# The first stretch of a two-block transformer kernel: gain row between the warming matmuls, x's second tile later in the queue, two casts on GpSimd, steps in the order of k-tile pairs

## The chip, the cores and the metric

The kernel runs on one core of a Trainium2 chip. The core has five engines with queues of their own: TensorE (PE in the profile, its weight loads PEld), VectorE (DVE), ScalarE (ACT), GpSimd (POOL) and SyncE (SP, which here only starts transfers). Sixteen DMA engines move data between HBM and the on-chip memory SBUF; matmul results go to PSUM. The metric is the device time of one execution in microseconds (us), lower is better.

## The reference

Two layers of one transformer block and one layer of another run over 256 tokens of width 1024, in float32. What the change touches is the very beginning, the norm of layer 0 and the first columns of its input product:

```
def rms_norm(x, g):
    xf = x.astype(jnp.float32)
    y = xf * lax.rsqrt(jnp.mean(xf * xf, axis=-1, keepdims=True) + RMS_EPS)
    return (y * g.astype(jnp.float32)).astype(x.dtype)
...
    for l in range(DEPTH):
        h = rms_norm(x, g_pre_mix[l])
        z = h @ w_in[l]
        q, k, v, cb, cc, cx, ga, gb = jnp.split(z, splits, axis=-1)
...
        mod = jax.nn.silu(c) @ w_cond[l] + b_cond[l]
```

After that come attention, a short convolution, gates, an output product and a feed-forward part per layer, then the second block, whose modulation `mod` is computed from `c` by DVE in gaps of the first block. None of that work is changed.

## The kernel before

**Numbers as two parts.** TensorE multiplies in the type float32r. To keep float32's accuracy, each operand is split into a rounded part H and a residue L = value - H. ACT makes H (a cast), DVE makes L (a subtraction). A product is H x H, H x L and L x H. So a weight of 128x1024 (a "raw" half, 512 KB) costs one transfer by SP, one cast on ACT, one subtraction on DVE, and on PE, per tile of 128 tokens, four matmuls for its H (against both parts of x) and two for its L.

**The weight stream.** All weights lie in one packed array in the order of use. `emit_raw` issues the next raw half; there are NRAW = 7 raw buffers, so that a transfer waits until the L of the half seven before has been computed. NSPLIT = 12 pairs of H and L are held.

**Order.** A scheduler (the Tile layer) puts each engine's instructions in a fixed order when the kernel is built, about in the order of the source, and adds the waits. Each engine then runs its queue in that order; what waits holds up everything behind it. `tc.issue_after(i)` puts an instruction behind another one in that order. In the first stretch, `q_first`, the helpers `A` and `V` chain all of ACT's and DVE's work in the order in which the source calls them.

**The first stretch.** It makes q of layer 0, 1024 columns in two halves c = 0 and 1, for the token tiles t = 0 and 1:

- PE starts with WARM = 13 matmuls on a tile of ones (`warm`), which compute nothing that is used. Then the gain row `g0` (one row of 1024) is spread over all partitions by a matmul with a column of ones (`gp`, in the trace g0p), then WARM2 = 4 more warming matmuls.
- `square` sums x squared, one half of the columns on ACT (c = 0), one on DVE (c = 1); `root` adds the two and takes the power -0.5 on POOL (rs_x); `scaled` multiplies x by it and by the gain row, in pieces (xg); `turned` transposes two k-tiles of 128 columns at a time on PE (pt), a pair; `putH` and `putL` make the pair's two parts (ACT, DVE).
- `halfH` and `halfL` make H and L of a raw half of the weights (Hq, Lq). For c = 0 there are four halves, Hq0 to Hq3, numbered (h, hf); the half (h, hf) goes with pair 2h + hf of x.
- `run(t, c, h, hf, j)` is a step of PE: j = 0 with the half's H (four matmuls of 512 columns), j = 1 with its L (two).

The second raw half is held back until x's first tile has landed: a copy of one column from x into its buffer (`state["gate"]`, on DVE) must come first. x's second tile is issued before it. The table `bcol` of the second block is fetched by ACT's queue; because of where `state["dma"]` stands its issue goes to the head of that queue.

Of the kernel before, what the change touches and what calls it, by code (L numbers as in the profile page):

```python
# [12 lines left out]
AF = mybir.ActivationFunctionType  # L13
ALU = mybir.AluOpType
# [20 lines left out]
WARM = 13  # L35
WARM2 = 4
# [126 lines left out]
def tile_model(ctx: ExitStack, tc: tile.TileContext, x_in, wpack, sink, convw, gains, c_in,  # L163
# [89 lines left out]
    def emit_raw():  # L253
        i, hf = divmod(state["raw"], 2)
        t = wp.tile([P, CH // 2], F32, tag="raw", name=f"raw{i}_{hf}", bufs=NRAW)
        if state["raw"] == 1:
            state["gate"] = nc.vector.tensor_copy(t[:, 0:1], xt[0][:, 512:513])
        state["dma"] = nc.sync.dma_start(t, wpack[i][:, hf * (CH // 2):(hf + 1) * (CH // 2)])
        raws[2 * i + hf] = t
        state["raw"] += 1  # L260
# [47 lines left out]
    warm = s2("warm", (P, 512), mybir.dt.bfloat16)  # L308
# [9 lines left out]
    pw = ps1("warm_ps")  # L318
    for i in range(WARM):
        mm(pw, warm[:, 0:P], warm, i == 0, i == WARM - 1)  # L320
# [3 lines left out]
    for i in range(WARM2):  # L324
        mm(pw, warm[:, 0:P], warm, i == 0, i == WARM2 - 1)
    for i in range(3):
        emit_raw()
    nc.sync.dma_start(xt[1], x_in[P:2 * P, :])
# [5 lines left out]
    with tc.issue_after(state["gate"].ins):  # L334
        state["v"] = nc.vector.tensor_copy(ident_r, ident)
# [32 lines left out]
    def rstd(ssq, name):  # L368
        rs = small("rs_" + name, 1)
        nc.gpsimd.tensor_tensor(rs, ssq[:, 1:2], nhalf, ALU.pow)  # L370
        return rs
# [331 lines left out]
    def q_first(q, xp):  # L703
# [51 lines left out]
        def halfH():  # L755
            n = state["spl"]
            while state["raw"] <= n:
                emit_raw()
            H = wp.tile([P, CH // 2], F32R, tag="H", name=f"Hq{n}", bufs=NSPLIT)
            L = wp.tile([P, CH // 2], F32R, tag="L", name=f"Lq{n}", bufs=NSPLIT)  # L760
            A(nc.scalar.copy, H, raws[n])
            HL.setdefault(n // 2, []).append((H, L))
            hl.append((H, L))
            state["spl"] += 1
# [7 lines left out]
        def run(t, c, h, hf, j):  # L772
# [5 lines left out]
            v = w[c, h][hf][j].rearrange("p (k c) -> p k c", k=2)  # L778
# [16 lines left out]
        scaled(0, root(0), (0, 256, 512, 1024))  # L795
        halfH()
        pt = [turned(0, i) for i in range(4)]
        for i in range(2):
            putH(0, i, pt[i])
            putL(0, i, pt[i])  # L800
        halfH()
        halfL(0)
        for i in range(2, 4):
            putH(0, i, pt[i])
            putL(0, i, pt[i])
        halfL(1)
        halfH()
        square(1, 0, False)
        square(1, 1, True)
        halfL(2)  # L810
        scaled(1, root(1), (0, 256, 512, 1024))
        halfH()
        w[0, 0] = get(("q", 0, 0, 0), 4)
        w[0, 1] = get(("q", 0, 0, 1), 4)
        run(0, 0, 0, 0, 0)
        run(0, 0, 0, 1, 0)
        run(0, 0, 0, 0, 1)
        run(0, 0, 1, 0, 0)
        run(0, 0, 0, 1, 1)
        run(0, 0, 1, 0, 1)  # L820
        run(0, 0, 1, 1, 0)
        pt = [turned(1, i) for i in range(4)]
        for i in range(4):
            putH(1, i, pt[i])
            putL(1, i, pt[i])
        halfL(3)
        state["behind"] = (state["a"], state["v"])
        for h in range(2):
            for hf in range(2):
                run(1, 0, h, hf, 0)  # L830
                if h == 0:
                    run(1, 0, h, hf, 1)
        run(0, 0, 1, 1, 1)
# [9 lines left out]
    def mixer1(l, xp, norms):  # L843
# [65 lines left out]
        for c in range(2):  # L909
            nc.scalar.activation(gt["ga"][c], gt["ga"][c], AF.Sigmoid)  # L910
            nc.scalar.activation(gt["gb"][c], gt["gb"][c], AF.Sigmoid)
            nc.vector.tensor_mul(yc[c], yc[c], gt["gb"][c])
            if l == 0 and c == 0:
                csb = s4("csb")
                nc.scalar.dma_start(csb, c_in[0].partition_broadcast(P))
                with tc.issue_after(state["dma"].ins):
                    nc.scalar.dma_start(bcol, b_cond)
# [298 lines left out]
```

## Time and profile before

| what | value |
|---|---|
| median of three runs | 1149.91 us (1148.66 to 1150.13) |
| the profiled execution's time | 1148.9 us |
| its span in the trace | 1146.9 us |
| granted clock of TensorE | 0.999 |
| PE busy | 1135.7 us |
| first matmul of the second half of q | 24.04 us from the span's start |

The span runs from the first to the last recorded instruction, so the execution's own time is 2.0 us longer. A row of the time line gives start and length in us, the engine, the line of the kernel, the operation, the tiles written <- read, partitions x elements and type, a count where equal rows are merged, and in brackets how long the engine stood idle before it and what ended that. "SPq" and "ACTq" are transfers being issued by those queues; the time from issue to landing is listed apart, by tensor.

### The profile page before, as it was taken

What the parts mean: (1) busy time and instruction counts of PE and PEld (TensorE: products, weight loads), DVE (VectorE), ACT (ScalarE), POOL (GpSimd) and SP (SyncE); (2) the same over time, 40 slices, a digit from 0 to 9 for tenths busy, and PEclk for the clock granted to TensorE, in tenths of its full rate; (3) what the DMA queues carried; (4) which work ended last, traced back from release to release, by engine and by line L of the source; (5) the groups of instructions that cost most, each with busy time, mean ns of one, the idle gap of its engine ahead of it and who ended that gap; (6) DMA issues with size and microseconds to landing.
All of it is one profiled execution on the core that took longest, in us unless ns stands there. A gap on an engine that the chain in (4) does not pass through costs nothing. (4 is left out here: it accounts for less than half of the span.)

```text
span 1146.9 us, 15965 instructions
## 1 busy us (share of the span) xinstructions
PE 1135.7 (99%) x5901; PEld 951.2 (83%) x5901; DVE 799.9 (70%) x1190; ACT 686.9 (60%) x1211; POOL 13.4 (1%) x28
## 2 busy tenths in 40 slices
PE   9999999999999999999999999999999999999997
PEld 5888888888888888888888888888888777888886
DVE  7888845858977647798864758867656747865652
ACT  6777866547654446688856557545455847645441
POOL 0000000000000000000000000000000000000000
PEclk9999999999999999999999999999999999999999
DMA  8934346737987752844565538987773653855610
GB/s 299 354 129 149 127 148 203 262 140 250 355 280 238 252 203 91 295 132 153 191 220 204 184 110 287 353 260 242 256 261 108 222 166 103 307 192 183 200 62 37
DMA packets 67039, 235.39 MB, mean 205 GB/s; under 512 B 8849, under 2 KB 9361, under 8 KB 66962
## 3 DMA queue, kind: packets, MB, share of 16 engines
q1 hardware_dynamic: 63216, 224.83, 57.4%
q10 hardware_dynamic: 3746, 9.56, 2.5%
q8 instruction: 46, 0.75, 0.3%
q14 instruction: 31, 0.25, 0.1%
HBM read 233.28 MB, written 1.07 MB: 204 GB/s over the span
## 5 line engine op out<-in xcount | busy, mean ns | idle before, releaser
L280 DVE TENSOR_TENSOR L<-raw,H 128x1024 fp32r<-128x1024 f32 x370 | 444.5, 1220 | 146.8 <-ACT H L278 139.4
L278 ACT CAST H<-raw 128x1024 fp32r<-128x1024 f32 x370 | 382.9, 1052 | 140.7 <-issue 39.1
L247 PE MATMUL dn<-H,fHL 128*128 128x512 f32 x432 | 116.1, 390 | 0.0
L247 PE MATMUL pu<-xf,H 128*128 128x512 f32 x432 | 108.2, 392 | 0.0
L247 PE MATMUL pg<-xf,H 128*128 128x512 f32 x432 | 107.8, 391 | 0.0
L247 PEld LDWEIGHTS dn<-H,fHL 128*128 128x128 f32 x432 | 79.8, 188 | 15.6
L247 PEld LDWEIGHTS pg<-xf,H 128*128 128x128 f32 x432 | 79.2, 188 | 15.2
L247 PEld LDWEIGHTS pu<-xf,H 128*128 128x128 f32 x432 | 77.7, 189 | 13.9
L524 DVE SCALAR_TENSOR_TENSOR raw<-raw,silu_c 128x1024 f32<-128x1024 f32 x48 | 58.2, 1218 | 29.3 <-DMA raw<-in_wpack_dram 29.3
L247 PE MATMUL dn<-L,fHL 128*128 128x512 f32 x216 | 66.6, 389 | 0.0
L247 PEld LDWEIGHTS pg<-xf,L 128*128 128x128 f32 x432 | 58.9, 190 | 4.2
L247 PEld LDWEIGHTS pu<-xf,L 128*128 128x128 f32 x432 | 58.9, 190 | 4.2
L247 PE MATMUL pu<-xf,L 128*128 128x256 f32 x432 | 60.2, 282 | 0.0
L247 PE MATMUL pg<-xf,L 128*128 128x256 f32 x432 | 60.2, 282 | 0.0
L247 PE MATMUL wo<-H,m 128*128 128x512 f32 x192 | 52.5, 395 | 0.0
L571 ACT CAST fHL<-f 128x512 fp32r<-128x512 f32 x27 | 16.8, 621 | 57.4 <-DVE f L569 57.4
L247 PEld LDWEIGHTS dn<-L,fHL 128*128 128x128 f32 x216 | 40.5, 188 | 8.6
L565 ACT ACTIVATE s<-s 128x512 f32<-128x512 f32 x27 | 17.1, 632 | 46.6 <-DVE s L458 46.5
L247 PEld LDWEIGHTS wo<-H,m 128*128 128x128 f32 x192 | 35.4, 188 | 7.6 <-issue 0.6
L247 PE MATMUL pcp<-H,y 128*128 128x512 f32 x128 | 35.2, 395 | 0.0
L247 PE MATMUL pap<-H,o 128*128 128x512 f32 x128 | 35.1, 394 | 0.0
L666 ACT ACTIVATE P<-S,nm 128x256 f32<-128x256 f32 x64 | 29.6, 480 | 8.9 <-DVE nm L660 6.4
(290 smaller groups left out, 1934.5 us busy)
## 6 DMA issues: line engine op xcount, KB each, us to landing
raw<-in_wpack_dram SPq DMA_DIRECT2D x422, 512.0 KB, 5.2
gpm<-in_gains_dram ACTq DMA_DIRECT2D x3, 512.0 KB, 6.8
gpf<-in_gains_dram ACTq DMA_DIRECT2D x3, 512.0 KB, 8.7
gqf<-in_gains_dram ACTq DMA_DIRECT2D x2, 512.0 KB, 6.6
out_dram<-x SPq DMA_DIRECT2D x4, 256.0 KB, 2.0
pmat<-in_pmat_dram SPq DMA_DIRECT2D x2, 384.0 KB, 6.9
x<-in_x_dram SPq DMA_DIRECT2D x2, 256.0 KB, 3.1
x<-in_x_dram SPq DMA_DIRECT2D x1, 512.0 KB, 6.8
```

Source lines behind the costliest of these rows:

```text
L247: nc.tensor.matmul(o, a, b, start=start, stop=stop, **kw)
L278: nc.scalar.copy(H, r)
L280: nc.vector.tensor_sub(L, r, H.bitcast(F32))
L524: nc.vector.scalar_tensor_tensor(w[u], w[u], 1.0, silu_c, ALU.mult, ALU.mult, accum_out=mcol[:, r, 2 * j + u:2 * j + u + 1])
L565: last = nc.scalar.activation(s, s, AF.Silu)
L571: nc.scalar.copy(fHL[:, 0], fv)
L666: nc.scalar.activation(Pt[:, hh, :], S[hh // 2][:, hh % 2, :], AF.Exp, bias=nm[:, hh:hh + 1], accum_out=den[:, hh:hh + 1])
```

## The change

- Ten and two warming matmuls instead of 13 and four, so that the gain row's matmuls come after the tenth. The tile of ones is 128 wide and is read four times instead of being 512 wide.
- The copy that holds back the second raw half goes from DVE to POOL. x's second tile is issued behind the second raw half instead of before it.
- `bcol` is fetched behind the last gate's sigmoid in layer 0 instead of at the start; the identity's cast to float32r comes at the end of the stretch.
- Hq1 and Hq3 are cast by POOL instead of ACT, Hq3 behind the second tile's power.
- The steps are written by pairs: the first H step stands between the transposes of pairs 1 and 2, all H steps of tile 0 and two of its L steps come before the second tile's transposes, the other two L steps after them. On ACT the square of the second tile goes ahead of pairs 2 and 3.

```diff
@@ -32,8 +32,8 @@
 NEG = -1e30
 CH = 2048
 
-WARM = 13
-WARM2 = 4
+WARM = 10
+WARM2 = 2
 NRAW = 7
 NSPLIT = 12
 LOOK = 3
@@ -254,7 +254,7 @@
         i, hf = divmod(state["raw"], 2)
         t = wp.tile([P, CH // 2], F32, tag="raw", name=f"raw{i}_{hf}", bufs=NRAW)
         if state["raw"] == 1:
-            state["gate"] = nc.vector.tensor_copy(t[:, 0:1], xt[0][:, 512:513])
+            nc.gpsimd.tensor_copy(t[:, 0:1], xt[0][:, 512:513])
         state["dma"] = nc.sync.dma_start(t, wpack[i][:, hf * (CH // 2):(hf + 1) * (CH // 2)])
         raws[2 * i + hf] = t
         state["raw"] += 1
@@ -305,7 +305,7 @@
         q.dma_start(g, gains[i].partition_broadcast(P))
         return g
 
-    warm = s2("warm", (P, 512), mybir.dt.bfloat16)
+    warm = s2("warm", (P, P), mybir.dt.bfloat16)
     nc.vector.memset(warm, 1.0)
     for c in range(2):
         nc.sync.dma_start(xt[0][:, c * 512:(c + 1) * 512], x_in[0:P, c * 512:(c + 1) * 512])
@@ -316,23 +316,25 @@
     ones = s2("ones")
     nc.vector.memset(ones[0:1, 0:P], 1.0)
     pw = ps1("warm_ps")
+    warm4 = warm.unsqueeze(1).to_broadcast([P, 4, P])
     for i in range(WARM):
-        mm(pw, warm[:, 0:P], warm, i == 0, i == WARM - 1)
+        mm(pw.rearrange("p (a c) -> p a c", a=4), warm, warm4, i == 0, i == WARM - 1)
     gp = [ps1(f"g0p{c}") for c in range(2)]
     for c in range(2):
         mm(gp[c], ones[0:1, 0:P], g0[0:1, HC[c]], True, True)
     for i in range(WARM2):
-        mm(pw, warm[:, 0:P], warm, i == 0, i == WARM2 - 1)
-    for i in range(3):
+        mm(pw.rearrange("p (a c) -> p a c", a=4), warm, warm4, i == 0, i == WARM2 - 1)
+    for i in range(2):
         emit_raw()
-    nc.sync.dma_start(xt[1], x_in[P:2 * P, :])
+    with tc.issue_after(state["dma"].ins):
+        state["dma"] = nc.sync.dma_start(xt[1], x_in[P:2 * P, :])
+    with tc.issue_after(state["dma"].ins):
+        emit_raw()
     nhalf = cst.tile([P, 1], F32, tag="nhalf", name="nhalf")
     nc.vector.memset(nhalf, -0.5)
     eps = cst.tile([P, 1], F32, tag="eps", name="eps")
     nc.vector.memset(eps, EPS)
     ident_r = cst.tile([P, P], F32R, tag="identr", name="ident_r")
-    with tc.issue_after(state["gate"].ins):
-        state["v"] = nc.vector.tensor_copy(ident_r, ident)
     modd = dr.tile([6, D], F32, tag="modd", name="modd")
     mcol = cst.tile([P, 6, KT], F32, tag="mcol", name="mcol")
     bcol = cst.tile([P, 6, KT], F32, tag="bcol", name="bcol")
@@ -367,7 +369,7 @@
 
     def rstd(ssq, name):
         rs = small("rs_" + name, 1)
-        nc.gpsimd.tensor_tensor(rs, ssq[:, 1:2], nhalf, ALU.pow)
+        state["pow"] = nc.gpsimd.tensor_tensor(rs, ssq[:, 1:2], nhalf, ALU.pow)
         return rs
 
     class Norm:
@@ -752,13 +754,16 @@
 
         hl = []
 
-        def halfH():
+        def halfH(pool=False):
             n = state["spl"]
             while state["raw"] <= n:
                 emit_raw()
             H = wp.tile([P, CH // 2], F32R, tag="H", name=f"Hq{n}", bufs=NSPLIT)
             L = wp.tile([P, CH // 2], F32R, tag="L", name=f"Lq{n}", bufs=NSPLIT)
-            A(nc.scalar.copy, H, raws[n])
+            if pool:
+                nc.gpsimd.tensor_copy(H, raws[n])
+            else:
+                A(nc.scalar.copy, H, raws[n])
             HL.setdefault(n // 2, []).append((H, L))
             hl.append((H, L))
             state["spl"] += 1
@@ -775,7 +780,7 @@
                 ps[t, c] = ps1(f"pq_0{c}{t}")
                 ps[t, c, "n"] = 0
             ts_ = slice(t * P, (t + 1) * P)
-            v = w[c, h][hf][j].rearrange("p (k c) -> p k c", k=2)
+            v = (w[c, h] if c else hl[2 * h:])[hf][j].rearrange("p (k c) -> p k c", k=2)
             first = ps[t, c, "n"] == 0
             ps[t, c, "n"] += 1
             for k in range(2):
@@ -792,44 +797,51 @@
         w = {}
         square(0, 0, False)
         square(0, 1, True)
-        scaled(0, root(0), (0, 256, 512, 1024))
+        rs = root(0)
+        scaled(0, rs, (0, 256, 512))
         halfH()
-        pt = [turned(0, i) for i in range(4)]
         for i in range(2):
-            putH(0, i, pt[i])
-            putL(0, i, pt[i])
-        halfH()
+            pt = turned(0, i)
+            putH(0, i, pt)
+            putL(0, i, pt)
+        run(0, 0, 0, 0, 0)
+        scaled(0, rs, (512, 1024))
+        halfH(True)
         halfL(0)
+        square(1, 0, False)
         for i in range(2, 4):
-            putH(0, i, pt[i])
-            putL(0, i, pt[i])
-        halfL(1)
-        halfH()
-        square(1, 0, False)
-        square(1, 1, True)
-        halfL(2)
-        scaled(1, root(1), (0, 256, 512, 1024))
-        halfH()
-        w[0, 0] = get(("q", 0, 0, 0), 4)
-        w[0, 1] = get(("q", 0, 0, 1), 4)
-        run(0, 0, 0, 0, 0)
+            pt = turned(0, i)
+            putH(0, i, pt)
+            putL(0, i, pt)
         run(0, 0, 0, 1, 0)
         run(0, 0, 0, 0, 1)
+        square(1, 1, True)
+        rs = root(1)
+        halfH()
+        halfL(1)
+        with tc.issue_after(state["pow"].ins):
+            halfH(True)
         run(0, 0, 1, 0, 0)
+        run(0, 0, 1, 1, 0)
         run(0, 0, 0, 1, 1)
-        run(0, 0, 1, 0, 1)
-        run(0, 0, 1, 1, 0)
+        scaled(1, rs, (0, 256, 512, 1024))
         pt = [turned(1, i) for i in range(4)]
         for i in range(4):
             putH(1, i, pt[i])
             putL(1, i, pt[i])
+            if i == 1:
+                halfL(2)
         halfL(3)
+        V(nc.vector.tensor_copy, ident_r, ident)
         state["behind"] = (state["a"], state["v"])
         for h in range(2):
             for hf in range(2):
                 run(1, 0, h, hf, 0)
                 if h == 0:
                     run(1, 0, h, hf, 1)
+        for h in range(2):
+            get(("q", 0, 0, h), 4)
+        run(0, 0, 1, 0, 1)
         run(0, 0, 1, 1, 1)
         run(1, 0, 1, 0, 1)
         run(1, 0, 1, 1, 1)
@@ -908,12 +920,12 @@
         drain()
         for c in range(2):
             nc.scalar.activation(gt["ga"][c], gt["ga"][c], AF.Sigmoid)
-            nc.scalar.activation(gt["gb"][c], gt["gb"][c], AF.Sigmoid)
+            sig = nc.scalar.activation(gt["gb"][c], gt["gb"][c], AF.Sigmoid)
             nc.vector.tensor_mul(yc[c], yc[c], gt["gb"][c])
             if l == 0 and c == 0:
                 csb = s4("csb")
                 nc.scalar.dma_start(csb, c_in[0].partition_broadcast(P))
-                with tc.issue_after(state["dma"].ins):
+                with tc.issue_after(sig.ins):
                     nc.scalar.dma_start(bcol, b_cond)
                 nc.scalar.activation(silu_c, csb, AF.Sigmoid)
                 nc.vector.tensor_mul(silu_c, silu_c, csb)
```

On SP the issues stand as follows before (from the second on; raw_0 and raw_1 are the two halves of a weight chunk, x_73 is its second tile):

```order
L258 DMA raw_0_106<-in_wpack_dram 128x1024
L328 DMA x_73<-in_x_dram 128x1024
L258 DMA raw_1_108<-in_wpack_dram 128x1024
L258 DMA raw_0_111<-in_wpack_dram 128x1024
L258 DMA raw_1_197<-in_wpack_dram 128x1024
```

and now:

```order
L258 DMA raw_0_101<-in_wpack_dram 128x1024
L258 DMA raw_1_103<-in_wpack_dram 128x1024
L330 DMA x_73<-in_x_dram 128x1024
L258 DMA raw_0_107<-in_wpack_dram 128x1024
L258 DMA raw_1_198<-in_wpack_dram 128x1024
```

x's tile moved behind the second raw half, the one that waits for the copy from x's first tile.

On ACT, from the first square on, before (with the tiles' numbers: jk and sx belong to the squares, Hq are weights, the x are the pairs of both tiles):

```order
L708 ACTIVATE jk_139,sx_135<-x_72 128x512
L708 ACTIVATE sx_135<-sx_135,eps 128x1
L708 CAST Hq_150<-raw_0_106 128x1024
L708 CAST x_165<-pt_153 128x2x128
L708 CAST x_168<-pt_156 128x2x128
L708 CAST Hq_171<-raw_1_108 128x1024
L708 CAST x_175<-pt_159 128x2x128
L708 CAST x_178<-pt_162 128x2x128
L708 CAST Hq_182<-raw_0_111 128x1024
L708 ACTIVATE jk_185,sx_136<-x_73 128x512
```

and now:

```order
L710 ACTIVATE jk_133,sx_129<-x_72 128x512
L710 ACTIVATE sx_129<-sx_129,eps 128x1
L710 CAST Hq_143<-raw_0_101 128x1024
L710 CAST x_149<-pt_146 128x2x128
L710 CAST x_155<-pt_152 128x2x128
L710 ACTIVATE jk_168,sx_130<-x_73 128x512
L710 ACTIVATE sx_130<-sx_130,eps 128x1
L710 CAST x_174<-pt_171 128x2x128
L710 CAST x_180<-pt_177 128x2x128
L710 CAST Hq_194<-raw_0_107 128x1024
```

The second tile's square (reading x_73) moved ahead of the casts of pairs 2 and 3, and Hq1 left the queue.

On POOL, after the fills at the start, before (rs_x are the two tiles' powers; ISA is an instruction that the scheduling layer inserts ahead of the first power):

```order
L1212 UNCONDITIONAL_BRANCH
L370 ISA
L370 TENSOR_TENSOR rs_x_145<-sx_135,nhalf 128x1
L370 TENSOR_TENSOR rs_x_192<-sx_136,nhalf 128x1
L370 TENSOR_TENSOR rs_apm_2504<-sa_pm_2476,nhalf 128x1
```

and now:

```order
L1224 UNCONDITIONAL_BRANCH
L257 COPY raw_1_103<-x_72 128x1
L372 ISA
L372 TENSOR_TENSOR rs_x_139<-sx_129,nhalf 128x1
L764 CAST Hq_164<-raw_1_103 128x1024
L372 TENSOR_TENSOR rs_x_192<-sx_130,nhalf 128x1
L764 CAST Hq_200<-raw_1_198 128x1024
L372 TENSOR_TENSOR rs_apm_2499<-sa_pm_2471,nhalf 128x1
```

The copy from x's first tile now stands ahead of the ISA instruction and the powers, and the two casts stand behind one power each.

## The prediction

> **What bounds the kernel now.** I read the page first, then the waits of TensorE (PE), then stretches of the first 60 us, then the first 25 us instruction by instruction. The page's first line, then four stretches (from:to, length, busy time with count of PE, PEld, DVE, ACT and POOL, granted clock, DMA share, GB/s):
>
> ```profile
> PE 1135.7 (99%) x5901; PEld 951.2 (83%) x5901; DVE 799.9 (70%) x1190; ACT 686.9 (60%) x1211; POOL 13.4 (1%) x28
> ...
> 0.00:8.99 8.99, 7.54 (x21) 2.74 (x22) 3.34 (x14) 3.35 (x5) 0.76 (x5) 1.00 0.77 259
> 8.99:16.80 7.81, 6.93 (x31) 4.76 (x30) 6.32 (x13) 5.04 (x10) 0.55 (x1) 1.00 1.00 385
> 16.80:24.04 7.24, 6.99 (x35) 5.72 (x34) 7.00 (x11) 6.58 (x11) 0.00 (x0) 1.00 0.69 238
> 24.04:60.00 35.96, 35.96 (x187) 30.50 (x186) 30.03 (x46) 27.26 (x40) 0.00 (x0) 1.00 0.92 338
> ```
>
> PE is busy 99% of the span, and from 24.04 us on without a break. So the change, which acts before that point, is worth exactly what it moves the start of the second column half of q (24.04 us), as long as weights, casts and residues stay ahead behind it. Before 24.04 PE is not full. Its rows (start, length, operation):
>
> ```profile
> 6.21 1.98 PE L247 MATMUL g0p<-g,ones 1*128 1x512 f32 x4
> 8.12 1.04 PE L247 MATMUL warm_ps<-warm 128*128 128x512 bf16 x4
> 8.99 1.04 PE L742 MATMUL pt<-ident,xg 128*128 128x128 f32 x8
> 15.30 0.74 PE L247 MATMUL pq<-Lq,x 128*128 128x512 f32 x2 [0.79 <-DVE Lq L713]
> 16.80 0.61 PE L742 MATMUL pt<-ident,xg 128*128 128x128 f32 x4
> 17.66 0.63 PE L742 MATMUL pt<-ident,xg 128*128 128x128 f32 x4 [0.25 <-DVE xg L713]
> 18.04 1.17 PE L247 MATMUL pq<-Hq,x 128*128 128x512 f32 x4
> 20.87 1.98 PE L247 MATMUL pq<-Hq,x 128*128 128x512 f32 x8
> 22.68 1.52 PE L247 MATMUL pq<-Lq,x 128*128 128x512 f32 x6
> 24.04 1.07 PE L247 MATMUL pq<-H,x 128*128 128x512 f32 x4
> ```
>
> From starts: eight H matmuls 20.87 to 22.68, so an H step (four) is 0.905; six L matmuls 22.68 to 24.04, so an L step (two) is 0.453. A group of eight transposes is 0.85 (8.99 to 9.84 by starts; 1.24 at 16.80, of which 0.25 waits); I take 1.0. The first half of q holds 8 H steps, 8 L steps and 16 transposes: 7.24 + 3.62 + 2.0 = 12.9 us. From 8.99 to 24.04 are 15.05, so about 2.2 us are idle or slow. That is all there is to fill behind the first transpose; ahead of it the whole start can move too.
>
> What feeds PE there: the transfers, and ACT, DVE and POOL.
>
> ```profile
> 1.65 0.43 SPq L258 DMA_DIRECT2D raw<-in_wpack_dram  x1
> 1.69 0.44 ACTq L917 DMA_DIRECT2D bcol<-in_b_cond_dram  x1
> 2.12 0.43 SPq L328 DMA_DIRECT2D x<-in_x_dram  x1
> 4.81 21.62 SPq L258 DMA_DIRECT2D raw<-in_wpack_dram  x15
> ```
>
> Median us from issue to landing for single issues: the first raw (at 1.65), x's tile two (at 2.12), the second raw (at 4.81); then the smallest, median and largest of the raws of the first 40 us.
>
> ```profile
> raw<-in_wpack_dram SPq DMA_DIRECT2D x1, 512.0 KB, 6.0
> x<-in_x_dram SPq DMA_DIRECT2D x1, 512.0 KB, 6.8
> raw<-in_wpack_dram SPq DMA_DIRECT2D x1, 512.0 KB, 5.4
> DMA to landing us min/median/max: 4.4/6.6/9.5
> ```
>
> So raw 0 lands at 7.65, x's tile two at 8.9, raw 1 at 10.2.
>
> ```profile
> 0.34 0.10 POOL L1205 MEMSET const-uint8-127<- 128x1 uint8 x1
> 0.91 0.48 DVE L309 MEMSET warm<- 128x512 bf16 x1 [0.91 <-PEq L1205]
> 4.62 0.15 DVE L257 COPY raw<-x 128x1 f32<-128x1 f32 x1 [3.06 <-DMA x<-in_x_dram]
> 4.83 0.23 DVE L335 CAST ident_r<-ident 128x128 fp32r<-128x128 f32 x1
> 4.97 0.68 DVE L713 SCALAR_TENSOR_TENSOR jk<-x 128x512 f32<-128x512 f32 x1
> 5.77 0.16 DVE L713 TENSOR_TENSOR sx<-sx 128x1 f32<-128x1 f32 x1
> 6.01 0.55 POOL L370 TENSOR_TENSOR rs_x<-sx,nhalf 128x1 f32<-128x1 f32 x1 [5.57 <-DVE sx L713]
> 7.43 1.54 DVE L713 SCALAR_TENSOR_TENSOR xg<-x,rs_x,g0p 128x256 f32<-128x256 f32 x3 [1.50 <-PE g0p L247]
> 7.67 1.05 ACT L708 CAST Hq<-raw 128x1024 fp32r<-128x1024 f32 x1 [3.11 <-DMA raw<-in_wpack_dram]
> 9.41 0.65 ACT L708 CAST x<-pt 128x256 fp32r<-128x256 f32 x2 [0.69 <-PE pt L742]
> 9.81 0.76 DVE L713 TENSOR_TENSOR x<-pt,x 128x256 fp32r<-128x256 f32 x2 [0.84 <-ACT x L708]
> 10.49 1.21 DVE L713 TENSOR_TENSOR Lq<-raw,Hq 128x1024 fp32r<-128x1024 f32 x1
> 12.69 0.64 ACT L708 ACTIVATE jk<-x 128x512 f32<-128x512 f32 x1
> 13.65 1.03 ACT L708 CAST Hq<-raw 128x1024 fp32r<-128x1024 f32 x1
> ```
>
> The first xg waits for the gain row's matmul (1.50), not for rs (ready at 6.56). The square of x's tile two starts at 12.69 without a wait: its data had been there since 8.9.
>
> **The change part by part.**
>
> *Warm-ups.* Three of 13 fall before the gain row, at 0.22 each by the second group (8.12 to 8.99, four): g0p starts at 5.55 instead of 6.21. The smaller memset brings PE's start 0 to 0.42 forward (0.48 down to no less than a 128x1 fill's 0.10, rounded); I take nothing. Then xg can start at 5.55 + 1.22 = 6.77 (7.43 less 6.21), the two later warm-ups end at 5.55 + 1.91 + 0.44 = 7.9, and the first transposes start there, 1.1 earlier than 8.99. rs must be ready at 6.7: without gate copy and identity cast in DVE's way the sum of squares starts at 4.62, 0.35 earlier, so rs comes at about 6.2.
>
> *What the early start reaches.* DVE's new order puts the second half of xg behind two residues: casts of pairs 0 and 1 at 7.9 + 0.42 = 8.3, residues at 8.7 to 9.5, the last xg piece to 10.2 (0.75), its transposes, and the cast of pair 2 at 10.65 at the earliest.
>
> *x's tile two, fourth.* Now it stands behind raw 1, which waits for a copy on POOL. That copy starts at 4.62 as DVE's did; between POOL's 128x1 rows (0.10 and 0.55) against DVE's 0.15, raw 1 is issued at 4.8 to 5.2, nearest 4.85. x follows 0.43 later, at 5.28. With the 5.4 of the raw issued at 4.81 it lands at 10.7; with 4.4 and 6.8 as ends, 9.65 to 12.45. Call it X. ACT now squares x ahead of the casts of pairs 2 and 3, so ACT stands still from about 8.9 to X, and with it everything behind in its queue: the sum of squares' second part, both casts, the third H.
>
> *The chain from X.* 0.96 on ACT (12.69 to 13.65), cast of pair 2 at X+1.0, residues 0.40 later and 0.76 long: X+2.15. DVE's square and sum 0.80 (4.97 to 5.77): X+2.95. POOL's power after 0.24, 0.55 long: X+3.75. Then the fourth H, cast by POOL: no row shows a 128x1024 cast there. Ends: 0.55 (POOL's 128x1 power) and 2.4 (twice DVE's two-operand 1.21); nearest in kind is ACT's same cast, 1.05, so I take 1.2. X+5.0. PE's H step on it, the L step of raw 1, the transposes of tile two: 0.905 + 0.453 + 1.0, X+7.4. Behind them stand 4 H and 6 L steps (before: 4 and 5), 3.62 + 2.72: the second half of q starts at X+13.75. xg of tile two is ready at about X+5.8 (behind L of raw 1, X+4.3) and does not add.
>
> X = 10.7 gives 24.45 against 24.04: **0.4 us later**. The other chain (cast of pair 2 at 10.65, so X replaced by 9.65) gives 23.4, so 0.65 earlier is the best this order allows with these durations.
>
> *At nothing:* bcol's issue (0.44 at 1.69) leaves an ACT that waits for x until 4.6 at worst anyway, and lies later beside a 60% busy ACT; ident_r's cast (0.23) moves behind the last L, before its first use by the key transposes; two casts fewer on ACT (2 x 1.05) free an engine that waits for X. Raw buffers come free later by 1 to 2 us; the second half needs one raw per 2.7 us of PE, and DMA then moves 338 GB/s, 1.6 us a raw. If that cover were gone, PE would wait in the stretch from 24.04, which has no wait now.
>
> [...] The power of tile two now starts 0.2 us after L of raw 1, a DVE operation with two SBUF inputs. In the one overlap here POOL was not held up, but there one input was in PSUM:
>
> ```profile
> 254.26 0.55 POOL L370 TENSOR_TENSOR rs_apm<-sa_pm,nhalf 128x1 f32<-128x1 f32 x1 [4.92 <-ACT sa_pm L365]
> 254.31 0.41 DVE L212 TENSOR_TENSOR xf<-pt_nf,xf 128x256 fp32r<-128x256 f32 x1
> ```
>
> The sum above goes by this row. [...]
>
> The profiled execution took 1148.9 (span 1146.9), 1.0 under the median of 1149.91. With 0.4 on top: 1149.3, or 1150.3 against the median. 0.2% (2.3 us) is about what a measurement of this kernel can tell from no change.
>
> **The rivals.**
>
> 1. *PE is filled.* If x lands about when it did (8.9) and POOL's casts take half of ACT's, PE could run from 7.9 nearly without a gap: 7.9 + 12.9 = 20.8, 3.2 earlier: **1146.7**. For it: all the earlier pieces are ready sooner. Against: the order on DVE and ACT alone holds the point to 23.4. It needs those chains to be shorter than their rows.
>
> 2. *POOL is held by DVE.* Power waits until L of raw 1 ends, X+4.3 instead of X+3.2, and the fourth H follows: 1.05 more, 25.5: **1151.4**.
>
> 3. *x lands early, the order decides:* 23.4, **1149.3**.
>
> 4. *Slower: what POOL does unseen.* Ahead of the first power POOL's queue holds an instruction (named ISA in the order) that the trace does not show. Before, it lies in POOL's 5.57 us of idle time, and the power starts 0.08 after the sum's end at 5.93. So it takes anything from 0 to 5.3. Now the gate copy stands ahead of it, and it cannot start before 4.85. Up to 1.3 it costs nothing, up to about 2.4 X hides it; beyond that each microsecond counts. At 5.3 rs is ready at 10.7 instead of 6.2, xg starts 3.95 later than 6.77, and the best chain goes from 23.4 to 27.4: 3.35 over 24.04, **1153.3**. For it: the instruction is there and moved behind a wait. Against: the power was not even 0.1 late at 6.01, which asks for a coincidence if it is long. [...]
>
> **How the numbers follow.** The forecast, X between its ends without hold: 0.42, **1150.3**, its own range 1149.3 to 1152.1. Held POOL 0.20, early x 0.12, filled PE 0.14, the unseen instruction 0.12. Faster by over 0.2% is the filled PE and a little of the early x: 0.16. Slower is the unseen instruction (long enough) and the top of the held one: 0.15. The rest is the same, 0.69. The range reaches halfway into the filled PE and to the unseen instruction's price: 1147.0 to 1153.2.
>
> **What would show it.** In the changed kernel's trace: g0p near 5.6 and the first transposes near 7.9; ACT idle before its second square, ended by DMA x, until about 10.7; POOL's two casts near 1.2; the second half of q near 24.5. Power of tile two starting only when L ends would show the second rival; the first power later than 7, the fourth. A square of tile two that does not wait, with PE dense from 8, makes me wrong on the fast side. Behind that point PE should stay without a wait to 60 us.

## The result and the profile after

In 20 runs of each, the kernel before took 1149.34 us (median; 1147.93 to 1152.12) and the changed one 1152.02 us (1149.39 to 1153.36): ratio 1.0020, 95% interval 1.0013 to 1.0027. The change makes the kernel slower, by 2.7 us between the medians and by 2.3 us (1.5 to 3.1) by the ratio, which is not the quotient of the medians here or below. The forecast was +0.4, and the time lies inside the range given. The profiled execution of the changed kernel took 1151.74 us and has a span of 1149.5 us (before 1146.9), with a mean granted clock of 0.996 (before 0.999).

First the page's line of busy times and the waits of PE over 0.7 us (us in total, times, longest), both of the changed kernel:

```profile
PE 1137.6 (99%) x5896; PEld 952.6 (83%) x5896; DVE 801.5 (70%) x1189; ACT 685.9 (60%) x1209; POOL 17.1 (1%) x31
```

```profile
PE pq L247 <- ACT Hq L710: 1.6, 1, 1.6
PE warm_ps L247 <- DVE warm L309: 1.1, 1, 1.1
PE pq L642 <- DVE qs L637: 0.8, 1, 0.8
PE pq L247 <- POOL Hq L764: 0.7, 1, 0.7
```

The first and the fourth are new, and both lie in the first half of q. Stretches of the first 60 us, cut where the working of the prediction cut them, the third at the start of the second half of q:

```profile
0.00:8.99 8.99, 7.69 (x23) 3.21 (x24) 3.10 (x14) 4.00 (x7) 1.46 (x6) 1.00 0.67 215
8.99:16.80 7.81, 5.36 (x18) 2.91 (x17) 6.38 (x11) 2.59 (x6) 3.50 (x3) 0.84 1.01 373
16.80:27.06 10.26, 10.26 (x41) 8.46 (x40) 7.42 (x11) 7.67 (x11) 0.00 (x0) 0.79 0.60 201
27.06:60.00 32.94, 32.94 (x167) 27.70 (x166) 27.75 (x43) 24.58 (x37) 0.00 (x0) 1.00 0.95 346
```

The second half of q starts at 27.06 instead of 24.04, 3.0 later, and PE is full behind it, as before. The spans differ by 2.6: nothing is added later, and some 0.4 is made up. Two things are new in these rows. From 8.99 to 16.80 PE works 5.36 us instead of 6.93. And the third number from the end, the granted clock, is 0.84 and 0.79, where before it was 1.00 everywhere. The rows of the time line in that stretch:

```profile
4.47 0.71 POOL L257 COPY raw<-x 128x1 f32<-128x1 f32 x1 [4.03 <-DMA x<-in_x_dram]
4.78 1.98 PE L247 MATMUL g0p<-g,ones 1*128 1x512 f32 x4
5.49 0.55 POOL L372 TENSOR_TENSOR rs_x<-sx,nhalf 128x1 f32<-128x1 f32 x1 [0.31 <-DVE sx L715]
5.58 0.43 SPq L330 DMA_DIRECT2D x<-in_x_dram  x1
7.13 0.60 PE L744 MATMUL pt<-ident,xg 128*128 128x128 f32 x4
9.05 1.04 POOL L764 CAST Hq<-raw 128x1024 fp32r<-128x1024 f32 x1 [3.01 <-DMA raw<-in_wpack_dram]
9.28 1.89 DVE L715 TENSOR_TENSOR Lq<-raw,Hq 128x1024 fp32r<-128x1024 f32 x1
10.34 0.63 ACT L710 ACTIVATE jk<-x 128x512 f32<-128x512 f32 x1 [2.14 <-DMA x<-in_x_dram]
12.36 0.68 DVE L715 SCALAR_TENSOR_TENSOR jk<-x 128x512 f32<-128x512 f32 x1
13.08 0.16 DVE L715 TENSOR_TENSOR sx<-sx 128x1 f32<-128x1 f32 x1
13.16 1.23 DVE L715 TENSOR_TENSOR Lq<-raw,Hq 128x1024 fp32r<-128x1024 f32 x1
13.32 1.48 POOL L372 TENSOR_TENSOR rs_x<-sx,nhalf 128x1 f32<-128x1 f32 x1 [3.23 <-DVE sx L715]
14.76 1.03 POOL L764 CAST Hq<-raw 128x1024 fp32r<-128x1024 f32 x1
15.84 2.07 PE L247 MATMUL pq<-Hq,x 128*128 128x512 f32 x4 [0.73 <-POOL Hq L764]
18.57 1.91 PE L744 MATMUL pt<-ident,xg 128*128 128x128 f32 x8
```

Read from the bottom. PE waits at 15.84 for the fourth H, which POOL casts from 14.76, because its power of 128 numbers took 1.48 us instead of 0.55 (the row at 5.49). In that time DVE computed L of raw 1 (13.16 to 14.39), which has two inputs in SBUF: the power ends 0.41 behind it. The same happens the other way round at 9.05: POOL casts until 10.09, and DVE's L, begun at 9.28, ends 1.08 later, after 1.89 instead of the 1.21 to 1.23 it takes alone. Then the last two rows: four H matmuls of 2.07 and eight transposes of 1.91, where at full clock they are 1.20 (e2 below, from 16.13) and 1.04 (before, from 8.99). The granted clock around them (again the third number from the end):

```profile
14.00:15.00 1.00, 1.00 (x4) 0.33 (x2) 0.56 (x2) 0.00 (x0) 1.00 (x2) 0.64 0.95 377
15.00:16.00 1.00, 0.27 (x2) 0.16 (x1) 1.00 (x3) 0.00 (x0) 0.79 (x1) 0.50 1.11 397
16.00:18.00 2.00, 2.00 (x5) 1.61 (x6) 0.36 (x1) 0.00 (x0) 0.00 (x0) 0.50 0.99 379
18.00:20.00 2.00, 2.00 (x9) 1.70 (x9) 0.36 (x1) 0.71 (x2) 0.00 (x0) 0.50 0.59 240
21.00:22.00 1.00, 1.00 (x5) 0.77 (x5) 1.00 (x3) 1.00 (x2) 0.00 (x0) 0.94 0.00 0
```

Taken as 1.00 up to the fall and 0.50 behind it, 0.64 is full clock for 0.28 of that microsecond, so it fell to half at 14.28; in the same way it rose at 21.12. From 15.84 the work left to the second half of q is 0.905 + 0.453 + 1.0 + 6.34 = 8.70 by the rows of before, and it took 11.22, 2.5 more. Not all of that is the clock's: in two runs below (e2 and e5) the same steps in the same order took 9.05 at full clock (16.13 to 25.18 and 16.05 to 25.10). So 2.2 us are the clock's in this execution, and without them the point would have been about 24.9, 0.85 over before.

So two theories stood: the **clock** (fewer warming matmuls and the new waits let the clock fall, and that is most of the loss), and the **chain** (x's landing, then ACT, DVE and a held POOL, set the end, whatever the clock does). Twelve further kernels were to tell them apart; they do so in part.

### The profile page after: what moved, and what is told of

The parts are those of the page before. It is cut to its first block, busy times and chain, and to the rows that moved or that the text cites. A ratio compares the mean times of both kernels' runs of the same rounds, so it can differ in the third digit from the quotient of the medians.

```text
span 1149.5 us, 15953 instructions
## 1 busy us (share of the span) xinstructions
PE 1137.6 (99%) x5896; PEld 952.6 (83%) x5896; DVE 801.5 (70%) x1189; ACT 685.9 (60%) x1209; POOL 17.1 (1%) x31
```

## The experiments

Each of the twelve was timed in 11 runs. "Over before" is the difference of the medians to the kernel before on the same chip in the same session (1149.34 to 1149.64 there). X is where the square of x's tile two starts. The last four columns are of the one profiled execution, whose own time stands first: it need not be near the median (in e4 it is 1.2 below it, in e6 and e12 1.5 and 1.7 above).

| kernel | median | over before | ratio, 95% interval | profiled execution | X | second half of q | recorded clock at 0.50 |
|---|---|---|---|---|---|---|---|
| changed | 1152.02 | +2.68 | 1.0020, 1.0013 to 1.0027 | 1151.74 | 10.34 | 27.06 | 14.3 to 21.1 |
| e1_fill | 1151.56 | +2.05 | 1.0021, 1.0012 to 1.0030 | 1151.18 | 11.29 | 25.82 | 8.0 to 11.5 |
| e2_x_early | 1151.73 | +2.22 | 1.0024, 1.0015 to 1.0033 | 1151.10 | 8.96 | 25.18 | 9.3 to 12.7 |
| e3_act_casts | 1150.25 | +0.74 | 1.0007, 0.9998 to 1.0016 | 1150.25 | 12.33 | 25.50 | 9.4 to 16.2 |
| e4_l_behind | 1150.07 | +0.56 | 1.0003, 0.9994 to 1.0012 | 1148.92 | 10.64 | 23.73 | 8.9 to 12.3 |
| e5_warm_back | 1151.56 | +1.92 | 1.0019, 1.0010 to 1.0027 | 1151.55 | 10.55 | 25.10 | none |
| e6_warm_alone | 1149.67 | +0.03 | 1.0002, 0.9993 to 1.0010 | 1151.20 | 13.75 | 25.36 | see below |
| e7_l_warm | 1149.11 | -0.53 | 1.0000, 0.9991 to 1.0009 | 1149.19 | 10.43 | 24.09 | none |
| e8_l_x_warm | 1149.19 | -0.45 | 0.9997, 0.9988 to 1.0006 | 1149.19 | 10.45 | 24.57 | none |
| e9_l_k128 | 1149.65 | +0.30 | 1.0001, 0.9992 to 1.0009 | 1148.76 | 10.67 | 23.78 | none |
| e10_l_x_k128 | 1148.81 | -0.54 | 1.0001, 0.9991 to 1.0010 | 1148.46 | 8.97 | 23.42 | none |
| e11_l_x_k128_w6 | 1149.31 | -0.04 | 1.0001, 0.9992 to 1.0010 | 1149.31 | 9.80 | 24.71 | none |
| e12_fill_warm | 1151.00 | +1.56 | 1.0014, 1.0005 to 1.0023 | 1152.68 | 12.59 | 27.18 | none |

**e1: fill PE's two waits.** Seven and five warming matmuls in the places where PE waits at 12 and 15:

```
+        fill(7)
         run(0, 0, 1, 0, 0)
+        fill(5)
         run(0, 0, 1, 1, 0)
```

> The changed kernel with 7 warming matmuls between the first L step of tile 0 and the H step on the third weight half, and 5 more ahead of the H step on the fourth; nothing else moves. Clock theory: PE's two gaps (1.64 and 0.73 us by its waits) let the granted clock fall to 0.50 from 15 to 21 us, and that costs 2.5 us. Then no stretch of the first 27 us is below clock 1.00, the second half of q starts at 15.84 + 0.905 + 0.453 + 1.0 + 6.34 = 24.5 instead of 27.06, and the time is 0.3 to 0.6 us above the kernel before, 2 to 2.5 below the changed one. Chain theory: the late x tile and the chain behind it cost the 2.7 us by themselves; then filling the gaps changes nothing, or costs a little more.

No fall of the clock behind 12 us any more, and yet only 0.6 less than the changed kernel's +2.68, with overlapping intervals. In the profile x landed 0.95 later, and the clock was at half before the filled places, from 8 us. So this run does not bear out the clock theory as stated: the waits between 12 and 16 are not the only place at which the clock falls. It does not refute it either, since the clock did fall, elsewhere.

**e2: x's tile two ahead of raw 1 again**, as in the kernel before:

```
-    for i in range(2):
-        emit_raw()
-    with tc.issue_after(state["dma"].ins):
-        state["dma"] = nc.sync.dma_start(xt[1], x_in[P:2 * P, :])
-    with tc.issue_after(state["dma"].ins):
+    for i in range(3):
         emit_raw()
+    nc.sync.dma_start(xt[1], x_in[P:2 * P, :])
```

> The changed kernel with x's second tile issued where it was, ahead of the second weight half; all else as changed. If the place of x's tile is the root: it lands at 8.9 instead of 10.3, ACT's second square does not hold up the casts of pairs 2 and 3, the third H is cast by 12.6 instead of 13.6, PE's gaps stay under 1.5 us, the clock stays at 1.00 and the second half of q starts at 22.6 to 23.4: 0.6 to 1.4 us faster than before. If the clock theory holds but the first gap (PE now waits longer for the second H, whose weights land at 10.2) is enough to drop it: slower than before by 1 to 2 us. If the place of the casts is the root: as the changed kernel, +2.7.

x no longer has to be waited for (its square starts at 8.96 without a wait), and nothing is won beyond the noise. The chain shifts to raw 1, which now lands later: POOL's cast of it holds DVE's L of raw 0 until 12.06, and DVE's queue goes on from there to the held power. (Part of the delay is the clock's, at half from 9.3 to 12.7.)

```profile
8.96 0.64 ACT L707 ACTIVATE jk<-x 128x512 f32<-128x512 f32 x1
9.95 1.04 POOL L761 CAST Hq<-raw 128x1024 fp32r<-128x1024 f32 x1 [3.62 <-DMA raw<-in_wpack_dram]
10.15 1.91 DVE L712 TENSOR_TENSOR Lq<-raw,Hq 128x1024 fp32r<-128x1024 f32 x1
13.45 1.22 DVE L712 TENSOR_TENSOR Lq<-raw,Hq 128x1024 fp32r<-128x1024 f32 x1
13.61 1.48 POOL L369 TENSOR_TENSOR rs_x<-sx,nhalf 128x1 f32<-128x1 f32 x1 [2.62 <-DVE sx L712]
16.13 1.20 PE L247 MATMUL pq<-Hq,x 128*128 128x512 f32 x4 [1.55 <-POOL Hq L761]
```

The fourth H step comes at 16.13, no earlier than in the changed kernel (15.84) although x landed at 8.6 instead of 10.3. x's place by itself is not the cause.

**e3: both casts on ACT again.** `halfH(True)` becomes `halfH()` at both places.

> The changed kernel with Hq1 and Hq3 cast by ACT again, at their places in the order. Port theory (POOL and a DVE operation with two SBUF inputs hold each other up): the first L takes 1.2 instead of 1.89, the second power 0.55 instead of 1.48, and the fourth H comes at about 14.6 instead of 15.8. With the clock theory the second gap of PE nearly closes; if the first gap (1.6) alone does not drop the clock, the second half of q starts at 23.5 to 24.0 and the time equals that of before within 0.5 us; if it does, the time is 1 to 2 us above. If the casts' place does not matter: +2.7 as the changed kernel.

The port theory, here and in e4, is the author's name for the hold in the changed kernel's rows at 9.28 and 13.32 (L 1.89 instead of 1.23, the power 1.48 instead of 0.55); that a port is behind it no run shows.

```profile
10.20 1.22 DVE L715 TENSOR_TENSOR Lq<-raw,Hq 128x1024 fp32r<-128x1024 f32 x1
15.31 1.47 POOL L372 TENSOR_TENSOR rs_x<-sx,nhalf 128x1 f32<-128x1 f32 x1 [9.22 <-DVE sx L715]
```

1.9 less than the changed kernel, with intervals that still overlap; as the clock fell, 1 to 2 over before was expected, and it is 0.74. L of raw 0 is back at 1.22, since no cast runs on POOL beside it. The expectation missed in one more point: the power still took 1.47, because L of raw 1 still stands ahead of it on DVE; but no cast queues behind the power on POOL any more. The clock was at half for longer than in any other run but the changed one (9.4 to 16.2), with x late at 12.33, and the time is still near before's. That speaks for the chain.

**e4: L of raw 1 behind xg of tile two on DVE.** One line moves (and the PE step that uses it):

```
         halfH()
-        halfL(1)
         with tc.issue_after(state["pow"].ins):
             halfH(True)
         run(0, 0, 1, 0, 0)
         run(0, 0, 1, 1, 0)
-        run(0, 0, 0, 1, 1)
         scaled(1, rs, (0, 256, 512, 1024))
+        halfL(1)
+        run(0, 0, 0, 1, 1)
```

> The changed kernel with the second L behind the second tile's xg on DVE, so that no operation with two SBUF inputs runs beside the second power (PE's order then has tile two's first transposes ahead of the fourth H step). Port theory: the second power takes 0.55 instead of 1.48, the fourth H is ready about 1 us earlier (14.8), and PE has transposes to do in the second gap. With the clock theory, if this keeps the clock up: second half of q at 23.5 to 24, equal to before within 0.6 us; if the first gap alone drops it, 1 to 2 us above before. If POOL was not held by DVE, the power takes 1.48 again and the time stays 2.7 above.

```profile
13.62 0.55 POOL L372 TENSOR_TENSOR rs_x<-sx,nhalf 128x1 f32<-128x1 f32 x1 [3.35 <-DVE sx L715]
14.13 1.04 POOL L764 CAST Hq<-raw 128x1024 fp32r<-128x1024 f32 x1
14.21 1.53 DVE L715 SCALAR_TENSOR_TENSOR xg<-x,rs_x,g0p 128x256 f32<-128x256 f32 x3 [0.67 <-POOL rs_x L372]
15.66 1.22 DVE L715 TENSOR_TENSOR Lq<-raw,Hq 128x1024 fp32r<-128x1024 f32 x1
23.73 1.07 PE L247 MATMUL pq<-H,x 128*128 128x512 f32 x4
```

The power is back at 0.55, the cast starts 0.63 earlier though x landed 0.3 later, and transposes can fill PE while the cast runs. POOL's cast beside xg is not held (1.04 at 14.13): xg reads x from SBUF and the gain row from PSUM. The time falls by 2.1 us, and the interval (up to 1.0012) no longer meets that of the changed kernel (from 1.0013). This is the largest single piece, by a little over e3's. It holds two things, which no run separates: the power that is no longer held (0.93), and PE's new order, with the transposes ahead of the fourth H step.

**e5: the warming matmuls of before** (WARM = 13, WARM2 = 4), all else as changed.

> The changed kernel with 13 and 4 warming matmuls again instead of 10 and 2 (0.66 us more ahead of the gain row, 0.44 us more behind it), all else as changed. Clock theory (fewer warming matmuls ahead of waits let the granted clock halve, in the first 12 us or in the gaps from 12 to 16): granted clock 1.00 from 8 to 12 us; the gaps behind 12 us stay, so a drop there is still possible; time 0.5 to 1.5 us under the changed kernel's 2.5 over before, so 1.0 to 2.0 over before, and runs that lie closer together. Wait theory (only the waits of x's place and of GpSimd count, the clock is a bystander): everything up to the second half of q starts 0 to 1.1 us later, time 2.5 to 3.5 us over before.

The recorded clock does not fall before 1148 us in this profile, and the second half of q comes at 25.10 = X + 14.55. The median is at the top of what the clock theory said, 0.8 less than the changed kernel with overlapping intervals. The second half's +1.06 is not all of this profile's loss: its span is 2.4 over before, and another 0.7 arises by 59 us (0.4 of it made up again) and 1.1 between 660 and 866 us, places that the change does not touch; 1.0 of the last is one wait of PE for DVE, of which e2, e6, e7, e10 and e12 show 0.3 to 0.5. That remains open. Nor does this profile stand for all eleven runs: by the mean clock of each run, five of them, at 0.997, are the five slowest (1152.35 to 1153.07), and the six at 0.998 to 1.000 lie between 1149.66 and 1151.56.

**e6: the warming part of the change alone**, in the kernel before (10 and 2 matmuls from the narrow tile).

> The kernel before with the warming part of the change alone (10 and 2 matmuls out of a 128-wide tile instead of 13 and 4). Clock theory: a drop of the granted clock to 0.50 between 8 and 12 us in the profile, 1.5 to 2 us of PE time lost where PE is full, time 0.5 to 1.5 us over before. Wait theory: the first transposes come up to 1.1 us earlier, the order of DVE and ACT behind them is as before: time 0 to 0.7 us under before, clock 1.00.

No difference in the median, against the clock theory's 0.5 to 1.5. The profiled execution was the slowest of its eleven (1151.20; the fastest 1148.05), and it shows why one must not read the clock from the granted clock alone:

```profile
5.43 3.77 PE L247 MATMUL g0p<-g,ones 1*128 1x512 f32 x4
9.14 1.03 PE L247 MATMUL warm_ps<-warm 128*128 128x512 bf16 x2
9.97 1.91 PE L743 MATMUL pt<-ident,xg 128*128 128x128 f32 x8
```

```profile
5.43:11.53 6.10, 6.10 (x16) 3.07 (x15) 2.57 (x8) 1.89 (x4) 0.55 (x1) 1.00 0.94 347
```

The four gain matmuls take 3.77 instead of 1.98, the transposes 1.91 instead of 1.04, which is half speed; the record says 1.00. PE had not come up to full speed by 5.43, and there is no record for the state in which it starts: the first entry in the trace's list of clock changes is a rise to full speed, here at 13.56 us, in the kernel before at 5.22 and in the changed one at 4.05. PE had been working without a stop from 1.05 to 13.56. So the mean clock of a run, too, leaves out what its start lost.

**e7: e4's order with 13 and 4 warming matmuls; e8: the same with x early.**

> The kernel with the residue of raw 1 behind xg of tile two (POOL's power 0.55, second half of q at 23.73) and 13 and 4 warming matmuls. Clock theory: no drop between 8 and 12 us, second half of q at 22.5 to 23.5, time 0.3 to 1.3 us under before. Wait theory: the warming costs 0 to 1.1 us of start, second half of q at 24 to 24.8, time 0.5 to 1.5 us over before.

> As the run before (residue behind xg of tile two, 13 and 4 warming matmuls), and x's tile two queued ahead of raw 1 again, as in the kernel before. Clock theory: no drop between 8 and 12 us; x lands at 9 instead of 10.3 to 12, the square of tile two does not wait, but raw 1 lands later, so the second half of q comes at 22.3 to 23.5, time 0.3 to 1.5 us under before. If x's place is worth something by itself, this run is 0.5 us or more under the one without it; if raw 1 then ends the wait, the two are within 0.4 us. Wait theory without the clock: within 0.5 us of before.

Both are where the kernel before is, and within 0.1 of each other: x's place is worth nothing here either. By the medians both meet the clock theory's times, by the ratios (1.0000 and 0.9997) they hardly do, and the second halves of q (24.09 and 24.57) come later than it said. e7 against e5 differs only in L's place and the PE step that uses it: 2.4 us less, intervals 0.9991 to 1.0009 against 1.0010 to 1.0027. That is the second time that this one move is worth 2 us, though in the two profiles the second half of q differs by 1.0 only. e7 against e4 differs only in the warming: 1.1 less, intervals overlap.

**e9: a gain row over 128 rows.** In e4 the clock fell at 8.9 although PE stood still for only 0.24 between 5.43 and 8.86. To see whether the gain row's matmuls, which contract over one row, have a part in that fall, they contract here over 128 rows, of which 127 are zero:

```
+    nc.gpsimd.memset(g0[:, HC[1]], 0.0)
+    nc.vector.memset(g0[:, HC[0]], 0.0)
     nc.scalar.dma_start(g0[0:1, :], gains[0:1, :])
...
-        mm(gp[c], ones[0:1, 0:P], g0[0:1, HC[c]], True, True)
+        mm(gp[c], ones[:, 0:P], g0[:, HC[c]], True, True)
```

> The kernel with the residue of raw 1 behind xg of tile two and 10 and 2 warming matmuls (1150.07, 0.56 over before, clock 0.50 from 8.9 to 12.3), with one thing more: the gain row's four matmuls contract over 128 rows (row 0 the gains, the others zeros) instead of one row. Same instructions on PE, same columns, same result. [...] Gap theory (only stops of PE count, a matmul is a matmul): the drop at 8 to 10 us stays in the profile or in half of the runs, time 1149.8 to 1150.4; the zeros and the later start of the gains' transfer could add up to 0.5.

No fall in the profile, and a median (1149.65) 0.15 under the gap theory's lowest, but only 0.26 nearer to before than e4's (+0.30 against +0.56); and one warming matmul of the later group now stands ahead of the gain row (11 there, 1 behind). This does not decide it.

**e10, e11: candidates.** e9 with x early, and that with 6 and 4 warming matmuls.

> As the run before, and x's tile two queued ahead of raw 1 as in the kernel before. [...] Gap theory: 1149.5 to 1150.2. If x's place matters by itself it is 0.4 us or more under the run before, otherwise within 0.3.

> As the run before with 6 and 4 warming matmuls instead of 10 and 2: the gain row's matmuls start at 3.6 to 4.2 if its transfer has landed. [...] Gap theory: PE stays or falls to half speed between 4 and 12 us, time 1150 or more.

e10 has the lowest median of all, 0.54 under before and 0.84 under e9, which would be x's place; but its ratio 1.0001 (0.9991 to 1.0010) is that of e9 and does not tell it from before. e11 is no better: all ten of its warming matmuls stand ahead of the gain row on PE, so that this still started only at 5.29, and the idea was not tried as meant. No version beat the kernel before by more than the measurement can tell.

**e12: both helps for the clock on the changed order**, 13 and 4 at the start and e1's filling.

> The changed order with both helps for the clock together: 13 and 4 warming matmuls at the start, and 7 and 5 warming matmuls in the two waits of PE between 12 and 16 us. Nothing is taken from the chain from x's landing over ACT, DVE and POOL (x fourth in the queue, power held by the residue). If the clock is what the order loses beyond that chain: clock 1.00 from 8 to 27 us in the profile, second half of q at x's landing + 14.2 to 14.6 (the changed kernel's chain at full clock), and the time 0.8 to 1.3 us over before, 0.6 to 1.1 under the run that has only the 13 and 4. If it is the chain alone: as that run, 1.7 to 2.1 over before.

```profile
8.00:27.00 19.00, 18.34 (x82) 11.85 (x81) 14.89 (x25) 10.23 (x20) 3.50 (x3) 1.00 0.77 272
```

```profile
11.49 1.04 POOL L764 CAST Hq<-raw 128x1024 fp32r<-128x1024 f32 x1 [5.68 <-DMA raw<-in_wpack_dram]
12.59 0.63 ACT L710 ACTIVATE jk<-x 128x512 f32<-128x512 f32 x1 [2.14 <-DMA x<-in_x_dram]
15.56 1.48 POOL L372 TENSOR_TENSOR rs_x<-sx,nhalf 128x1 f32<-128x1 f32 x1 [3.04 <-DVE sx L715]
27.18 0.39 PE L799 MATMUL pq<-H,x 128*128 128x512 f32 x1
```

The clock is 1.00 from 8 to 27 us and PE hardly stands still (18.34 of 19.00, the filling counted), and the second half of q comes even later than in the changed kernel, at 27.18 = X + 14.59, since x landed at 12.59 in this execution, the second slowest of the eleven. The median, +1.56, is between the two expectations, and the interval lies above 1; the mean clock is 0.998 or 0.999 in all eleven runs. So, as far as the record shows the clock, the order loses without it: +1.6 of the +2.7 remain with both helps in.

## Why the prediction was right, and where it was not

The side of the forecast, slightly slower, and the range were right. The likeliest case was not: it took POOL unheld and gave +0.4, and the chance for a loss of more than 0.2% was put at 0.15 against 0.69 for no clear change, where 0.20% was measured. That the time lies inside the range is in part luck. +2.7 is more than the forecast's own upper end (+2.2, with x's latest landing) and more than a held POOL (+1.5); the range reached on to +3.3 for the unseen instruction of GpSimd, which cost nothing. What stood in its place in the profiled execution were the hold and the clock: with the measured X of 10.34 the forecast's sum gives 24.09, the chain took 0.8 more than the sum and the clock 2.2, which makes 27.06.

- **The start.** g0p came at 4.78 (forecast 5.55), the first transposes at 7.13 (7.9): PE's first matmul was 0.4 earlier, which I had priced at nothing, and PE reached full speed earlier (at 4.05 instead of 5.22 by the trace's list of clock changes). That the early start does not set the end held: e7, with its transposes 1.9 later than the changed kernel, is faster.
- **The gate copy** took 0.71 on POOL, over my upper end of 0.55; x was issued at 5.58 (5.28). DVE's square of the same tile, with both inputs in SBUF, ran beside it from 4.44 to 5.13, so this may be the same hold as at the second power; no run separates the two. x landed 4.7 later, X = 10.34 (10.7). In the eight profiles with x in fourth place that landing took 4.7, 4.7, 4.8, 4.8, 5.1, 6.0, 6.7 and 7.2 us: my ends of 4.4 to 6.8 were nearly the real spread, and X went up to 12.59.
- **The chain from X** was followed step by step: sum of tile two begun at X + 2.74 (forecast 2.95), power begun at X + 2.98 (3.19), cast of 1.03 (1.2). The term that failed is the power: 0.55 in the sum, 1.48 in fact. I had gone by the row of one overlap, in which DVE read one input from PSUM, and there the power was first besides (254.26 against 254.31), so that the row could not show a power being held that starts behind DVE's operation; the rival "POOL is held by DVE" had the hold and nearly its price (1.05; it is 0.93). The traces show it in both directions, each time with two SBUF inputs on DVE and the second of the two taking longer (L behind the cast at 9.28: 1.89 instead of 1.23; the power behind L at 13.32: 1.48 instead of 0.55; the cast behind L in e1: 1.53 instead of 1.03), and they show a pair that is not held (e4's cast beside xg, which reads PSUM: 1.04).
- **Behind the fourth H** the forecast had X + 13.75. At full clock the runs with this order gave X + 14.55 (e5), 14.53 (e1, at full clock behind 12 us) and 14.59 (e12), and the changed kernel, without the clock's 2.2, X + 14.55 as well. The difference of 0.8 is the hold's 0.93, less 0.2 each for the earlier power and the shorter cast, plus 0.35 for the steps behind the fourth H (9.05 in place of 8.70), but for rounding. With L behind xg it was X + 13.1 (e4, e9), and X + 13.66 in e7, where DVE's queue is later from the start on. So the chain was right up to the hold, and the order that makes the hold costs 0.9 (e7 against e5) to 1.4.
- **The clock** had no term at all. The sum took each matmul at full speed because the trace of before showed 1.00 in all its stretches; filling or losing PE time was priced as waiting alone. In the profiled run it doubled whatever PE did from 15.84 to 21.1: +2.2. How much of the median's +2.7 it is cannot be said: e12 and e5, whose profiles are without it, keep +1.6 and +1.9 with intervals that overlap the changed kernel's, and e6 shows no loss clear of the noise from fewer warming matmuls alone. The mean clock of the changed kernel's 20 runs does not settle it: the eight at 0.999 or 1.000 have a median of 1152.3, the six at 0.995 or 0.996 one of 1151.9, so a recorded fall does not pick out the slow ones.
- **The other rivals.** A filled PE: no, it waited 1.64 and 0.73. Early x: no, ACT waited 2.14 for it, and e2, with x early, is no faster. The unseen instruction ahead of the first power: the power starts at 5.49, 0.08 behind the sum's end and 0.31 behind the gate copy's, so it costs nothing. (That it could take 5.3 at most does not follow from the row, whose idle time is 5.57; nothing hangs on it.)
- **At nothing** stayed at nothing: the moved cast of ident_r and bcol's issue show no waits, and PE has none from 27.06 to 60. Two casts fewer on ACT freed an engine that waited, as said.

## What to carry to other kernels

Before an instruction goes to GpSimd, look at what VectorE does in the same microseconds: here a two-input VectorE operation out of SBUF ahead of a tiny GpSimd one turned its 0.55 us into 1.48, and putting that operation behind the next ones on VectorE, with the TensorE step that uses it, was worth two microseconds (2.1 in e4, 2.4 in e7 against e5). In a start-up phase the clock of TensorE needs a term of its own: it stayed at half for 3.4 or 6.8 us more in five of the fourteen profiles, and what set that off was not found. Read the spread of the landing times as a range of the end, not as one value. And a chain of steps from one landing, summed from the rows, came within 0.3 us of the runs once the hold was in it (X + 14.8 by the second rival, 14.53 to 14.59 measured), with errors of 0.2 to 0.35 in single steps that partly cancelled.

## What the runs showed of the hardware that was not expected

- Half clock came in pieces of one length. From the shares in the microsecond rows, the stretches last 3.42 us in e1, e2 and e4 and 6.84 in the changed kernel and 6.82 in e3, once or twice 3.42. In the changed kernel, cut at that length, the piece before the fall has PE busy for 1.78 of 3.42, the first piece at half has 2.69 and was followed by another, the second is full and was the last. The two rows behind them are the first pieces at half of e1, which was the only one, and of e3, which was followed by another:

```profile
10.86:14.28 3.42, 1.78 (x8) 0.94 (x7) 2.87 (x7) 2.08 (x6) 0.96 (x1) 1.00 0.99 389
14.28:17.70 3.42, 2.69 (x7) 1.58 (x6) 1.64 (x4) 0.00 (x0) 1.51 (x2) 0.50 1.02 386
17.70:21.12 3.42, 3.42 (x13) 2.92 (x12) 1.48 (x3) 1.73 (x5) 0.00 (x0) 0.50 0.43 177
8.04:11.46 3.42, 2.96 (x8) 2.01 (x8) 2.55 (x4) 0.62 (x3) 1.31 (x1) 0.50 1.00 376
9.42:12.83 3.41, 3.02 (x9) 2.14 (x10) 2.00 (x3) 1.54 (x2) 0.00 (x0) 0.50 1.01 377
```

  PE's busy time alone does not tell which piece is the last: 2.96 of 3.42 was enough in e1, 3.02 of 3.41 was not in e3. What sets the length of a piece, and which is the last, no run shows.

- The fall does not need a long standstill. In e4 the piece before it was busy for 3.19 of 3.42, 1.91 of them the gain row's matmuls on one row:

```profile
5.43:8.86 3.43, 3.19 (x12) 1.47 (x11) 1.28 (x4) 1.69 (x3) 0.55 (x1) 1.00 0.68 197
```

  In e1 the piece before the fall (4.62 to 8.04), with the same matmuls in it, was busy for 3.40 of 3.42. Nor does a wait have to bring a fall: e5 had waits of 0.90 and 1.12 between 12 and 16 us and kept its clock. What brings a fall was not settled (e9); the gain row's matmuls alone do not decide it, since in the changed kernel they lie between the rise at 4.05 and 7.46, one piece later, and no fall followed there.
- The start at half speed can last long. In e6 PE was busy from 1.05 to 13.56, without a stop, before the clock rose; in the other thirteen profiles it rose between 4.05 and 6.91.
- GpSimd's cast of 128x1024 takes 1.03 to 1.04 us, as ACT's does (1.05), against the 2.4 I had as an upper end; beside L it took 1.53 (e1).
